# A state-space scan with its chunk states packed by group: 128x256 states, products as two half matmuls

## The chip, the cores and the metric

One Trainium2 chip, one of its NeuronCores. The metric is the device time of one execution of the whole program in microseconds, lower is better. The engines are named as in the profile: PE (TensorE matmul) and PEld (its weight load), DVE (VectorE), ACT (ScalarE), POOL (GpSimd), SP (SyncE, which issues the DMAs).

## The reference, cut to what matters

The reference is a two-layer block of a generator: adaLN-modulated norm, one input projection for four parallel mixers (attention, short convolution, pooling, a bidirectional state-space scan), a gated merge, an output projection, and a gated ConvFFN. 512 latent and 256 context tokens, 1024 channels, all in float32. The change lies in the scan over chunks of 128 tokens (8 heads of 64 channels in 2 groups of 4, a state of 64 per group):

```python
def ssd_scan(x, dt, a_rate, bm, cm, h0):
    ...
    decay_to_end = jnp.exp(a_cum[..., -1:] - a_cum)
    states = jnp.einsum('bcsgn,bcgrs,bcsgrp->bcgrpn', bc, decay_to_end, xdt)
    chunk_decay = jnp.exp(a_cum[..., -1])

    def step(h, inp):
        st, dec = inp
        return h * dec[..., None, None] + st, h
    ...
    y_off = jnp.einsum('bclgn,bcgrpn,bcgrl->bclgrp', cc, h_prev, jnp.exp(a_cum))
    y = (y_diag + y_off).reshape(b, l, nh, p)
```

Each group has its own `bc` and `cc` (64 values per token) and its own four heads: a state of group 0 meets only `cc` of group 0.

## The kernel before, in words

Activations lie with channels on partitions and tokens along the free axis. Every projection (`mm`, lines 124 to 138) is made of three fp32r matmuls per 128 channels, high and low halves of both operands, in segments of 512 latent and 256 context tokens; the 128x1024 weight tiles are fetched by SP and split by ACT and DVE (`split`, line 93).

A layer runs in stages: attention beside the projections of the other mixers, then the scan (`ssd_main`, line 758) beside the merge of the three finished branches, then the scan's gate and norm (`ssd_gate`), then the merge of the scan's branch, the output projection and the ConvFFN. Layer 0 has context and latent outputs, layer 1 latent outputs alone. `interleave` (line 46) writes the two programs of a stage alternately: after each step of the scan it writes as much merge work as the step's `yield` states (10 or 9 us). The tile framework then orders the instructions of every engine by a timeline of its own, so neighbours in the program need not be neighbours on an engine. Every engine runs its list in order.

The scan has two parts. `ssd_chunk` (line 685) makes what lies within a chunk: `cb` (lines 690 to 693, one f32 matmul per group with 64 rows, the partitions of that group), the decays `e` from masks that POOL multiplies (`pm`), and `y`. `ssd_dir` (line 726), once for each direction and in lockstep, carries the state `hs` from chunk to chunk:

- `st` (line 744) is `bt` of the chunk (128 tokens by 128 columns: two groups of 64) times `xe` (128 tokens by 512: all heads), one f32 128x512 matmul. Of its four blocks of 64x256 two are wanted, group 0 with heads 0 to 3 and group 1 with heads 4 to 7; the others mix groups.
- `hs` (lines 745 to 754) is a 128x512 tile that POOL sets to zero; then, for each group, DVE takes the wanted 64x256 block, decays the old state and adds the new one. The zeros stand in the blocks that mix groups.
- `yo` (line 734) is `cT` of the chunk (128 rows, both groups) times `hs`, one f32 128x512 matmul, in which the zeros keep the groups apart. DVE scales it by `ex` into `yot` and adds that to `y`.

There are 10 `st` and 10 `yo` in layer 0, 10 and 8 in layer 1. `yo` shares the two PSUM buffers of tag `a` with `e`, `st` the two of tag `b` with `cb`.

Of the kernel before, what the change touches and what calls it, by code (L numbers as in the profile page):

```python
# [15 lines left out]
P = 128  # L16
# [13 lines left out]
# columns of the packed constants  # L30
C_ID, C_ONE, C_LE, C_GE, C_GT, C_LT, C_EDGE = 0, 128, 256, 384, 512, 640, 768
C_N = 768 + 4 * 2 * 8
# columns of a layer's packed per-channel parameters
Q_NM, Q_NF, Q_CS, Q_FC, Q_XW, Q_XB, Q_PS, Q_SN, Q_BM = 0, 8, 16, 28, 160, 178, 184, 188, 192
Q_N = 192 + 48
# columns of a layer's packed row parameters
# [9 lines left out]
def interleave(main, side):  # L46
    """Trace main; after each of its steps trace as much of side as the TensorE time (us) that the step leaves free."""
    owed = 0.0
    for want in main:
        owed += want  # L50
        while owed > 0:
            got = next(side, None)
            if got is None:
                break
            owed -= got


def mixed(main, side, start, every):
    """main with a step of side after each `every` of its steps from the `start`th on, then the rest of side."""
# [7 lines left out]
class Kernel:  # L67
# [3 lines left out]
    # ---------------------------------------------------------------- helpers  # L71
# [21 lines left out]
    def split(self, hi, lo, src):  # L93
        """src = hi + lo, each of them exact in float32r."""
# [16 lines left out]
    def banks(self, **bufs):  # L111
        """The PSUM banks of a phase: mm for the projections, the other tags for what runs beside them."""
# [11 lines left out]
    def mm(self, w, mov, segs):  # L124
        """w.T @ mov for each token segment: [(first token, tokens, PSUM [P, tokens])]."""
# [17 lines left out]
    def transposes(self, src, tiles, exact=False, tag="b"):  # L143
        """Blocks of P columns of src, each transposed: [(first block, blocks, PSUM [P, blocks * P])].

        exact: src holds float32r values, which one pass moves."""
# [23 lines left out]
    def rows_rstd(self, pool, chunks, n, inv, eng=None, rb=None, ss=None):  # L170
        """1/rms over the channels (chunks on partitions), the same on every partition: PSUM [P, n]."""
# [53 lines left out]
    # ------------------------------------------------------------- modulation  # L225
    def first_norm(self):
        """h of the first layer: its shift on TensorE (the weights stationary), its scale on VectorE."""
# [66 lines left out]
    def mod_steps(self, l, p, conds, pool, bufs=2):  # L294
        """One modulation part on VectorE: rows of the weight scaled per partition and summed, then across partitions."""
# [30 lines left out]
    # -------------------------------------------------------------- attention  # L326
# [13 lines left out]
    def token_major(self, l, mt, segs, ap_):  # L340
        """A projected tile of P channels, transposed: [(first token tile, tiles, PSUM)]."""
# [7 lines left out]
    def heads_ready(self, l, mt, segs, tabs, ap_):  # L349
        """A projected pair of heads, token-major, RMS-normed, gained and rotated: SBUF [P, tiles * 2 heads, 64]."""  # L350
# [803 lines left out]
```

## Time and profile before

| | |
|---|---|
| device time, 3 runs | 2596.28, 2597.34 (median), 2598.14 us |
| span of the profiled execution | 2597.0 us, 34788 instructions (its device time is not listed apart from the three) |
| PE busy | 2520.1 us (97%) |
| PEld | 2144.5 us (83%) |
| DVE | 1684.6 us (65%) |
| ACT | 1002.4 us (39%) |
| POOL | 102.3 us (4%) |
| mean granted TensorE clock | 0.989 |

The profile shows one execution. Busy shares are means over all stages. A matmul's record begins when its weights or columns begin to go in, and the records of consecutive matmuls overlap, so what a matmul costs PE is read from the distance between the starts of records, not from their durations. An f32 matmul leaves two records, an fp32r one a single record. The chain of waits follows the work that ended last back through what released it; the waits say which engine an instruction waited for.

### The profile page before, as it was taken

The page shows a single profiled execution, that of the slowest core. Times are in us where ns is not written, and L with a number is a line of the kernel's source. Part 1 is how long each engine was busy: PE and PEld are TensorE (multiplying, and loading weights), DVE is VectorE, ACT ScalarE, POOL GpSimd, SP SyncE. Part 2 cuts the span into 40 slices and gives each one's busy share as a digit, 9 for nine tenths or more (in the row PEclk, how much of TensorE's full clock was granted, in tenths as well). Part 3 has the DMA queues.
Part 4 walks back from the last instruction along what each step waited for, and adds up shares of the span by engine and source line. Part 5 has one row for each costly group of instructions (what it writes and reads, how often), then busy time and mean ns, then how long its engine had stood idle before and what let it go on. Part 6 is the DMA issues. An engine that isn't in the chain of part 4 may idle for free.

```text
span 2597.0 us, 34788 instructions
## 1 busy us (share of the span) xinstructions
PE 2520.1 (97%) x13684; PEld 2144.5 (83%) x13684; DVE 1684.6 (65%) x2857; ACT 1002.4 (39%) x1717; POOL 102.3 (4%) x125
## 2 busy tenths in 40 slices
PE   7999999999999999999999989999999999899998
PEld 4878888887888888888888878888777788788887
DVE  5666564568689667787765576666478544655656
ACT  3465555431312233232223344665542333333332
POOL 0000000242000000000000000000042000000000
PEclk9999999999999999999999999999999999999999
DMA  6212222331566242344432242132332533233232
GB/s 234 66 33 96 68 68 80 93 105 42 170 196 195 83 138 73 114 152 140 143 111 73 68 144 66 39 104 94 98 106 77 179 110 105 69 107 98 89 102 70
DMA packets 92819, 272.21 MB, mean 105 GB/s; under 512 B 9968, under 2 KB 15600, under 8 KB 91504
## 3 DMA queue, kind: packets, MB, share of 16 engines
q1 hardware_dynamic: 92656, 269.99, 32.4%
q8 instruction: 108, 1.77, 0.3%
q14 instruction: 55, 0.45, 0.1%
HBM read 248.71 MB, written 21.23 MB: 104 GB/s over the span
## 4 chain that ended last, share of the span: by engine, by line
PE 89%; DVE 5%; DMA 2%; ACT 2%; issue 1%; SPq 0%; DVEq 0%; ACTq 0%
PE mm L134 26%; PE mm L135 26%; PE mm L136 26%; PE tp L152 3%; PE s L434 2%; PE ov L449 2%; PE modrow L274 1%; DVE wl L73 1%; ACT wh L95 1%; DMA braw<-bout 1%; PE yo L734 1%; PE st L744 1%; PE e L714 1%; PE y L721 0%; DMA wraw<-w_out 0%
## 5 line engine op out<-in xcount | busy, mean ns | idle before, releaser
L134 PE MATMUL mm<-hh,wh 128*128 128x512 f32 (+1 forms) x2648 | 946.9, 358 | 7.4 <-ACT hh L208 5.9
L135 PE MATMUL mm<-hl,wh 128*128 128x512 f32 (+1 forms) x2648 | 945.7, 357 | 1.4 <-DVE hl L76 1.3
L136 PE MATMUL mm<-hh,wl 128*128 128x512 f32 (+1 forms) x2648 | 941.4, 356 | 1.4 <-DVE wl L73 1.4
L95 ACT CAST wh<-wraw 128x1024 fp32r<-128x1024 f32 (+5 forms) x384 | 350.9, 915 | 748.3 <-PE mm L135 635.5
L73 DVE TENSOR_TENSOR wl<-wraw,wh 128x1024 fp32r<-128x1024 f32 (+5 forms) x384 | 411.9, 1073 | 280.2 <-ACT wh L95 275.3
L134 PEld LDWEIGHTS mm<-hh,wh 128*128 128x128 f32 x2648 | 503.4, 190 | 81.1 <-ACT hh L208 8.0
L135 PEld LDWEIGHTS mm<-hl,wh 128*128 128x128 f32 x2648 | 503.2, 190 | 72.6 <-issue 3.1
L136 PEld LDWEIGHTS mm<-hh,wl 128*128 128x128 f32 x2648 | 502.9, 190 | 72.4 <-DVE wl L73 3.2
L76 DVE SCALAR_TENSOR_TENSOR fc<-mm,par,fc 128x511 f32<-128x511 f32 (+1 forms) x264 | 172.9, 657 | 64.0 <-ACT fc L490 61.3
L134 PE MATMUL mm<-ah,wh 128*128 128x512 f32 (+1 forms) x576 | 196.8, 343 | 2.4 <-ACT ah L95 1.0
L135 PE MATMUL mm<-al,wh 128*128 128x512 f32 (+1 forms) x576 | 196.5, 342 | 0.9 <-DVE al L73 0.9
L136 PE MATMUL mm<-ah,wl 128*128 128x512 f32 (+1 forms) x576 | 196.2, 342 | 0.0
L76 DVE SCALAR_TENSOR_TENSOR x<-mm,mod,x 128x512 f32<-128x512 f32 (+1 forms) x128 | 80.1, 632 | 118.7 <-PE mm L136 118.5
L76 DVE SCALAR_TENSOR_TENSOR macc<-mraw,cond,macc 128x1024 f32<-128x1024 f32 x112 | 141.0, 1280 | 12.9 <-DMA mraw<-w_modk 12.8
L136 PE MATMUL mm<-bh,wl 128*128 128x512 f32 (+1 forms) x384 | 137.4, 359 | 1.7 <-DVE wl L73 1.6
L135 PE MATMUL mm<-bl,wh 128*128 128x512 f32 (+1 forms) x384 | 138.5, 361 | 0.4 <-DVE bl L73 0.4
L134 PE MATMUL mm<-bh,wh 128*128 128x512 f32 (+1 forms) x384 | 137.9, 361 | 0.2 <-ACT bh L95 0.2
L134 PEld LDWEIGHTS mm<-ah,wh 128*128 128x128 f32 x576 | 110.3, 192 | 15.7 <-ACT ah L95 1.4
L490 ACT ACTIVATE fc<-mm,par 128x512 f32<-128x512 f32 (+1 forms) x132 | 80.8, 612 | 109.4 <-PE mm L136 109.4
L135 PEld LDWEIGHTS mm<-al,wh 128*128 128x128 f32 x576 | 110.6, 192 | 13.2 <-DVE al L73 1.4
L136 PEld LDWEIGHTS mm<-ah,wl 128*128 128x128 f32 x576 | 110.3, 192 | 12.1
L73 DVE TENSOR_TENSOR pt<-tp,pt 128x256 fp32r<-128x256 f32 (+1 forms) x144 | 76.9, 540 | 52.9 <-ACT pt L95 51.4
(253 smaller groups left out, 2921.2 us busy)
## 6 DMA issues: line engine op xcount, KB each, us to landing
wraw<-w_up SPq DMA_DIRECT2D x88, 512.0 KB, 3.5
mraw<-w_modk SPq DMA_DIRECT2D x80, 512.0 KB, 3.9
wraw<-w_in SPq DMA_DIRECT2D x64, 512.0 KB, 3.5
wraw<-w_gate SPq DMA_DIRECT2D x64, 512.0 KB, 3.5
wraw<-w_branch SPq DMA_DIRECT2D x64, 256.0 KB, 2.9
wraw<-w_down SPq DMA_DIRECT2D x40, 320.0 KB, 3.0
wraw<-w_out SPq DMA_DIRECT2D x24, 512.0 KB, 3.5
mraw<-w_modm SPq DMA_DIRECT2D x8, 1024.0 KB, 11.2
```

Of the source, the lines that this page charges most:

```text
L73: return (eng or self.nc.vector).tensor_tensor(out=out, in0=in0, in1=in1, op=op)
L76: return self.nc.vector.scalar_tensor_tensor(out=out, in0=in0, scalar=scalar, in1=in1, op0=op0, op1=op1)
L95: self.nc.scalar.copy(hi, src)
L134: self.nc.tensor.matmul(out, lhsT=a, rhs=x0, start=(k == 0), stop=False)
L135: self.nc.tensor.matmul(out, lhsT=a, rhs=x1, start=False, stop=False)
L136: self.nc.tensor.matmul(out, lhsT=b, rhs=x0, start=False, stop=(k == nk - 1))
L152: self.nc.tensor.transpose(tp[:, j * P : (j + 1) * P], src(lo + j), self.identr if exact else self.ident)
L274: nc.tensor.matmul(rows[:32, p * 256 : (p + 1) * 256], lhsT=cond[:, k], rhs=raws[b][:, k, p * 256 : (p + 1) * 256], start=(k == 0), stop=( ...
L434: nc.tensor.matmul(sc[:, t0 : t0 + n], lhsT=qT[:, h, i * P : (i + 1) * P], rhs=self.kT[g][:, part, t0 : t0 + n], start=(part == 0), stop=( ...
L449: nc.tensor.matmul(ov, lhsT=self.v[:, kc, g].rearrange("p a d -> p (a d)"), rhs=pt[j][:, c].rearrange("p h q -> p (h q)"), start=(j == 0 a ...
L490: nc.scalar.activation(o, s, AF.Copy, scale=w1)
L714: nc.tensor.matmul(e, lhsT=self.maskr[:, d * P : (d + 1) * P], rhs=pm.rearrange("p h q -> p (h q)"), start=(n == 0), stop=(n == 3))
```

## The change

The state of a direction becomes 128x256: group 0 on partitions 0 to 63, group 1 on 64 to 127, with no zeros. The product `st` becomes two matmuls, one per group, with 64 output columns and 256 columns of `xe`, into the two partition halves of one PSUM tile. `yo` becomes two matmuls of 64 rows and 256 columns, each into a PSUM buffer of its own. POOL's memset goes. The state's decay and addition are one DVE instruction each of 128x256 where there were two of 64x256; `yot` is made by two of 128x256 where there was one of 128x512. The decays are copied once per layer into `eg`, in which each partition half holds its own group's (`ssd_decays`, two small ACT copies). Comments and docstrings also went from the file; empty lines stand in their place, so that line numbers behind `ssd_chunk` are shifted.

```diff
+    def ssd_decays(self, sp):
+
+        self.eg = sp.tile([P, 2, 6, 4], F32, name="eg", tag="eg", bufs=1)
+        for g in range(2):
+            r = slice(64 * g, 64 * g + 64)
+            self.nc.scalar.copy(self.eg[r], self.ex[r, 4:6, :, 4 * g : 4 * g + 4])
+
     def ssd_dir(self, l, d, with_ctx, sp):
...
             if hs is not None and (with_ctx or c < 4):
-                yo = self.aux("a", 512, "yo")
-                nc.tensor.matmul(yo, lhsT=self.cT[:, c * P : (c + 1) * P], rhs=hs, start=True, stop=True)
+                yo = [self.aux("a", 256, "yo") for _ in range(2)]
+                for g in range(2):
+                    r = slice(64 * g, 64 * g + 64)
+                    nc.tensor.matmul(yo[g], lhsT=self.cT[r, c * P : (c + 1) * P], rhs=hs[r], start=True, stop=True)
                 t = sp.tile([P, 512], F32, name="yot", tag="es", bufs=2)
-                self.tt(self.heads(t), self.heads(yo), self.bc(self.ex[:, d, c]), ALU.mult)
+                for g in range(2):
+                    ex = self.ex[:, d, c, 4 * g : 4 * g + 4]
+                    self.tt(self.heads(t[:, 256 * g : 256 * g + 256]), self.heads(yo[g]), self.bc(ex), ALU.mult)
                 self.tt(self.y[:, c], self.y[:, c], t, ALU.add)
...
-            st = self.aux("b", 512, "st")
-            nc.tensor.matmul(st, lhsT=self.bt[:, c], rhs=xe, start=True, stop=True)
-            new = sp.tile([P, 512], F32, name="hs", tag=f"hs{d}", bufs=2)
-            nc.gpsimd.memset(new, 0.0)
+            st = self.aux("b", 256, "st")
             for g in range(2):
-                r, q = slice(64 * g, 64 * g + 64), slice(256 * g, 256 * g + 256)
-                if hs is None:
-                    nc.vector.tensor_copy(new[r, q], st[r, q])
-                else:
-                    dec = self.ex[r, 4 + d, c, 4 * g : 4 * g + 4]
-                    self.tt(new[r, q].rearrange("p (h e) -> p h e", e=64), hs[r, q].rearrange("p (h e) -> p h e", e=64), dec[:, :, None].to_broadcast([64, 4, 64]), ALU.mult)
-                    self.tt(new[r, q], new[r, q], st[r, q], ALU.add)
+                r = slice(64 * g, 64 * g + 64)
+                nc.tensor.matmul(st[r], lhsT=self.bt[:, c, r], rhs=xe[:, 256 * g : 256 * g + 256], start=True, stop=True)
+            new = sp.tile([P, 256], F32, name="hs", tag=f"hs{d}", bufs=2)
+            if hs is None:
+                nc.vector.tensor_copy(new, st)
+            else:
+                self.tt(self.heads(new), self.heads(hs), self.bc(self.eg[:, d, c]), ALU.mult)
+                self.tt(new, new, st, ALU.add)
             hs = new
...
         for c in (4, 5, 0, 1, 2, 3) if with_ctx else range(4):
             self.ssd_chunk(l, c, sp)
             yield 10.0
+        self.ssd_decays(sp)
         for _ in zip(*[self.ssd_dir(l, d, with_ctx, sp) for d in range(2)]):
             yield 9.0
```

How the instructions stand on PE, in layer 0's scan. Rows give line, operation, output<-inputs, shape; `mm` are the merge's projections, x2 is two in a row. First the middle of the scan, before:

```order
L134 MATMUL mm<-hh_101,wh 128x256
L135 MATMUL mm<-hl_102,wh 128x256
L734 MATMUL yo<-hs,cT 128x512
L744 MATMUL st<-xe,bt 128x512
L136 MATMUL mm<-hh_101,wl 128x256
L134 MATMUL mm<-hh_103,wh 128x256
```

The same place after the change:

```order
L136 MATMUL mm<-hh_103,wl 128x256
L760 MATMUL st<-xe,bt 64x256 x2
L746 MATMUL yo<-hs,cT 128x256
L134 MATMUL mm<-hh_105,wh 128x256
L135 MATMUL mm<-hl_106,wh 128x256
L136 MATMUL mm<-hh_105,wl 128x256
L134 MATMUL mm<-bh,wh 128x512
L746 MATMUL yo<-hs,cT 128x256
L135 MATMUL mm<-bl,wh 128x512
```

The two halves of `st` stand together, the two of `yo` with four projections between them. Over the whole program 16 of the 20 `st` pairs stand together and 4 have another matmul between their halves; of the 18 `yo` pairs none stands together. In eight places an `st` half or pair stands directly beside a `yo` half, as here. A little further on in layer 0 a split `st` pair, after the change:

```order
L134 MATMUL mm<-bh,wh 128x256
L135 MATMUL mm<-bl,wh 128x256
L760 MATMUL st<-xe,bt 64x256
L746 MATMUL yo<-hs,cT 128x256
L760 MATMUL st<-xe,bt 64x256
```

A half of `yo` has come between the halves of `st`; its partner stands further down.

## Rows read from the trace of the kernel before

**Rows 1.** The page: span, and PE's busy time with its instructions.
```profile
span 2597.0 us, 34788 instructions
...
PE 2520.1 (97%) x13684; PEld 2144.5 (83%) x13684; DVE 1684.6 (65%) x2857; ACT 1002.4 (39%) x1717; POOL 102.3 (4%) x125
```

**Rows 2.** The page: the chain that ended last, shares of the span by line.
```profile
PE mm L134 26%; PE mm L135 26%; PE mm L136 26%; PE tp L152 3%; PE s L434 2%; PE ov L449 2%; PE modrow L274 1%; DVE wl L73 1%; ACT wh L95 1%; DMA braw<-bout 1%; PE yo L734 1%; PE st L744 1%; PE e L714 1%; PE y L721 0%; DMA wraw<-w_out 0%
```

**Rows 3.** Stretches: length, busy us of PE, PEld, DVE, ACT, POOL; clock, DMA share, GB/s.
```profile
580.00:660.00 80.00, 80.00 (x413) 63.17 (x412) 66.58 (x122) 17.90 (x37) 18.47 (x20) 1.00 0.18 54
1950.00:2020.00 70.00, 68.80 (x287) 51.07 (x286) 60.06 (x100) 17.87 (x31) 15.59 (x16) 1.00 0.25 72
```

**Rows 4.** PE's waits, 1895 to 2150 us: who for whom, total, times, longest.
```profile
PE mm L136 <- DVE wl L73: 1.6, 1, 1.6
PE st L744 <- DVE xe L73: 1.2, 1, 1.2
```

**Rows 5.** Timeline of SP, layer 1: scan's result stored, first load of the next merge.
```profile
2057.86 0.46 SPq L786 DMA_DIRECT2D bout<-gt  x1
...
2099.61 0.33 SPq L808 DMA_DIRECT2D braw<-bout  x1
```

**Rows 6.** Timeline of PE, layer 0, around one `st`: start, length, tile, shape.
```profile
590.15 0.28 PE L136 MATMUL mm<-hh,wl 128*128 128x256 f32 x1
590.27 1.02 PE L744 MATMUL st<-xe,bt 128*128 128x512 f32 x2
590.72 0.68 PE L134 MATMUL mm<-hh,wh 128*128 128x256 f32 x1
591.24 0.28 PE L135 MATMUL mm<-hl,wh 128*128 128x256 f32 x1
```

**Rows 7.** The tile `yo`: count, duration in ns (min/median/max), first and last start.
```profile
L734 PE MATMUL yo<-hs,cT x36: 590/591/594, 610.3 to 2015.5; 128*128 128x512 f32 x36
L73 DVE TENSOR_TENSOR yot<-yo,ex x18: 683/688/693, 618.3 to 2016.9; 128x512 f32<-128x512 f32 x18
```

**Rows 8.** Timeline of PE, layer 0, around a lone `cb` of 64 rows.
```profile
520.72 0.28 PE L136 MATMUL mm<-bh,wl 128*128 128x256 f32 x1
520.92 0.49 PE L693 MATMUL cb<-cT,bT 64*128 64x128 f32 x2
521.34 0.50 PE L714 MATMUL e<-pm,maskr 128*128 128x512 f32 x1
```

**Rows 9.** Timeline of PE, fp32r matmuls with 32 output columns beside a full one.
```profile
52.81 0.39 PE L570 MATMUL mm<-hh,wd 128*32 128x512 f32 x1
53.04 0.39 PE L134 MATMUL mm<-hh,wh 128*128 128x512 f32 x1
```

**Rows 10.** Timeline of PE, layer 0, around two `cb` directly behind each other.
```profile
499.22 0.28 PE L136 MATMUL mm<-hh,wl 128*128 128x256 f32 x1
499.43 0.49 PE L693 MATMUL cb<-cT,bT 64*128 64x128 f32 x4
499.85 0.73 PE L714 MATMUL e<-pm,maskr 128*128 128x512 f32 x2
```

**Rows 11.** Timeline of PE behind f32 matmuls with 32 output columns.
```profile
49.85 1.89 PE L274 MATMUL modrow<-mraw,cond 128*32 128x256 f32 x8
51.67 0.39 PE L134 MATMUL mm<-hh,wh 128*128 128x256 f32 x1
51.90 0.39 PE L570 MATMUL mm<-hh,wd 128*32 128x512 f32 x1
```

**Rows 12.** The tile `hs`: count, duration in ns (min/median/max), first and last start.
```profile
L73 DVE TENSOR_TENSOR hs<-hs,ex x32: 406/422/1261, 593.5 to 2000.0; 64x256 f32<-64x256 f32 x32
L73 DVE TENSOR_TENSOR hs<-hs,st x32: 401/419/426, 605.7 to 2010.5; 64x256 f32<-64x256 f32 x32
L746 POOL MEMSET hs<- x20: 524/526/531, 488.8 to 1996.1; 128x512 f32 x20
L750 DVE COPY hs<-st x8: 409/422/428, 591.4 to 1957.1; 64x256 f32<-64x256 f32 x8
```

## The prediction, made before the changed kernel ran

> **What bounds the kernel now.** I read the page first: PE is busy for 97% of the span [rows 1], and in the chain of waits three quarters of the span are the projections of `mm`, while the two matmuls that are edited hold 1% each [rows 2]. The table of stretches then covers the two places where the chunk scan runs (580 to 660 us in layer 0, 1950 to 2020 us in layer 1): PE is busy for 80.0 of 80 and for 68.8 of 70 us, at a granted clock of 1.00, and VectorE for 83% and 86% [rows 3]. Beside the scan PE always has projections of the merge to run, so the scan is paid for in PE time and not in latency. Two views bear that out. PE's waits: from 1895 us on it waited 1.6 us once for a weight's low half and 1.2 us once for `xe`, both VectorE [rows 4]; in layer 0's scan stretch there is no wait. And the scan's result is stored in layer 1 by 2058 us but first read at 2099.6 us [rows 5], 41 us later, so a later chain of states delays nobody. What counts is how much PE time the same work takes after the edit.
>
> **What a state or output product costs now.** It is one f32 128x512 matmul, in the trace two records. Between the matmul record before `st` at 590.27 and the first regular one after it at 591.24 lie 0.97 us; 0.12 of that is the 128x256 `mm` that came in between (590.15 to 590.27 is that shape's step), so 0.85 us for 512 columns [rows 6]. A record of `yo` lasts the same 0.59 us [rows 6, 7]. There are 20 `st` (40 records in pairs) and 18 `yo` [rows 7]: 17.0 + 15.3 = 32.3 us of PE. Per 256 columns that is 0.43 us, per 128 it is 0.21.
>
> **The change, part by part.**
>
> **Output products.** Each becomes two matmuls with 64 rows and 256 columns, 0.43 us of columns each. The trace has such half-height matmuls already: `cb`, 64 rows by 128 columns. Alone between full-height ones, it starts 0.20 us after the record at 520.72 (0.12 is usual, so 0.08 late), the next record starts at 521.34 and lasts 0.50 us [rows 8] where 0.39 is usual [rows 9]. So 521.34 - 520.72 - 0.12 + 0.11 = 0.61 us for a product with 0.21 us of columns: 0.40 us goes into changing to half height and back. Two `cb` directly behind each other go from 499.22 to 499.85, with 0.73 us for the two records behind them [rows 10] (usual is 0.23 + 0.39 = 0.62 [rows 9]): 0.63 - 0.12 + 0.11 = 0.62 us for both. They run side by side, and the second costs nothing. A pair of `yo` halves side by side would thus take 0.43 + 0.40 = 0.83 us, against 0.85 now: even the best case gains nothing. But the order of the change shows that none of the 18 pairs stays together; full-height matmuls stand between the halves in every one. So each of the 36 halves pays alone: 36 x 0.83 = 29.9 against 15.3 us, **+14.6 us**. That is the term on which the forecast rests; its price is from eight `cb` that stand alone, all within 0.01 us.
>
> **State products.** Each becomes two matmuls with 64 output columns, one per half of the PSUM partitions. In the order 16 of 20 pairs stand together, 4 are split. Two prices are unknown. First, switching: after the f32 `modrow` with 32 output columns, eight records of 256 columns (8 x 0.21 = 1.71 us) begin at 49.85, and the next record begins 1.82 us later, 0.11 late, and then takes 0.23 us to the following one instead of 0.12 [rows 11]: 0.2 us to leave. The way in has no clean row; I take 0.14 (the same drain and half the weight columns), 0.34 in all. The ends: nothing, since fp32r matmuls with 32 output columns pass to a full one at the usual step of 0.23 us [rows 9], and 0.40 as for `cb`. I take 0.34, as `modrow` is f32 like `st`. Second, whether the two run side by side. No row has two column halves; the nearest is the `cb` pair [rows 10], which does, so I take 0.43 us for a pair; the other end is 0.85. The sum: 24 groups (16 pairs, 8 lone halves) x (0.43 + 0.34) = 18.5 against 17.0 us, **+1.5 us**. One after the other it would be +8.3, without a switching cost -6.7. The Trainium skill ("TensorE: Matmul & The Clock Gate", section "Measured speedup vs the span model") gives 2.38 times for three column tiles; my estimate from that is some 13% more than one for a pair, which would add 0.9 us to the sum, and no run here shows it.
>
> In eight places a lone `st` half or pair and a `yo` half stand directly beside each other, and one of the two changes is saved: 8 x 0.2 = **-1.6 us**.
>
> **VectorE.** The 32 decays and 32 additions of 64x256 become 16 and 16 of 128x256, at the 0.42 us that a 256-wide one takes now, and the 8 copies become 4 [rows 12]: -15.1 us. The 18 `yot` of 0.688 us [rows 7] become 36 of 256 columns, estimated at the same 0.42: +2.7. So 12.4 us less, over two layers, on an engine that PE waits for little. What it can give back is the 2.8 us of rows 4; PE also comes later at these places, so I take half, **-1.4 us**, with 0 and -2.8 as ends.
>
> **The rest at nothing.** 20 memsets of 0.53 us leave POOL [rows 12]; PE took none of its waits from them. Two small ScalarE copies (`eg`) come in each layer before the scan of the states; ScalarE is busy for 18 of 70 to 80 us there [rows 3], and uncovered they would cost about 1 us. No DMA is added; those that shift wait for the scan's end, with the 41 us of rows 5.
>
> **Sum:** 14.6 + 1.5 - 1.6 - 1.4 = +13.1 us on a span of 2597.0; the median of the runs, 2597.3, lies 0.3 us above that. **2610.4 us**, 0.5% slower. About 0.2% (5.2 us) is what a measurement can tell from no change.
>
> **The rivals.**
> - *Column halves run one behind the other.* +6.8 us for 16 pairs: 2617. For it: no row shows two of them at once. Against: `cb`.
> - *Column halves switch for free*, as the fp32r rows do [rows 9]: 24 x 0.34 = -8.2, less the shared changes that then fall away (+1.6): 2604. Against: `modrow` is the f32 case [rows 11].
> - *No difference to be measured.* Free switching, both VectorE waits gone (1.4 us more) and a lone `yo` half 0.1 us cheaper than rows 8 make it (36 x 0.1): 2610.4 - 6.6 - 1.4 - 3.6 = 2599. Against: three errors in one direction.
> - *Faster: halves run side by side at no price of change.* Then 20 and 18 products drop from 0.85 to 0.43 us each, -16 us, 2581. It decides from the point where split halves still overlap and a change costs less than 0.42 - 5.2 / 38 = 0.28 us. Rows 8 speak against the first and the written order against the second. The Trainium skill ("TensorEngine Tiling (Array Packing)", section "Theoretical Speedup") gives up to 2 times for such halves; by that rule the kernel would gain, and the same page's "Key Properties" has the drain at a mode change that rows 8 price.
> - *A new wait.* A `yo` pair now takes both PSUM buffers of tag `a`, which the `e` of the chunks use too; PE stops in order until VectorE has read a half (0.42 us). At 36 halves and up to 0.4 us each, +14 more: 2625. Against: projections stand between most pairs, and VectorE has less to do than before.
>
> **How the numbers follow.** Forecast (2605 to 2615): 0.57. One behind the other (to 2620): 0.17. Free switching (2601 to 2605): 0.10. No difference: 0.07. Faster: 0.04. New wait (above 2620): 0.05. The range 2601 to 2620 holds 0.84 of it. Slower by over 0.2%, beyond 2602.5: 0.57 + 0.17 + 0.05 + most of the free switching, 0.86; within 0.2%: 0.10; faster: 0.04.
>
> **What would show it.** Right: in the trace after, a lone `yo` half with about 0.08 us before it, and a record behind it that takes 0.10 us longer than usual; from the matmul before to the second one after, 0.8 us more than their own steps. `st` pairs whose four records come as two pairs of starts a few ns apart (side by side), or at four separate times (one behind the other). VectorE's busy time down by about 12 us while the span grows. Wrong: `yo` halves without a gap before them, or VectorE as the engine that PE waits for in the scan stretches, with more than 5 us in its waits.

## The result, and the profile after

The changed kernel takes 2616.27 us (median of 4 runs, 2611.88 to 2620.61), against 2597.74 (2596.28 to 2598.99) for the kernel before beside it: 18.5 us longer by the medians; the ratio with its 95% interval is 1.0078 [1.0064, 1.0091]. The forecast was 13.1 us longer, 2610.4 with a range of 2601 to 2620. The sign held, and the time lies in the range, though above the band of 2605 to 2615 that the forecast kept for itself; the size fell short by 5 us. Medians and ranges in this document leave out four executions (one of the changed kernel, two of variants, one of the kernel before) that took 2817 to 6410 us.

The page of the changed kernel, span and engines:

```profile
span 2618.7 us, 34868 instructions
...
PE 2536.9 (97%) x13760; PEld 2145.7 (82%) x13760; DVE 1670.8 (64%) x2839; ACT 1004.3 (38%) x1721; POOL 94.8 (4%) x105
```

Beside [rows 1] the span grows by 21.7 us and PE's busy time by 16.8, while VectorE loses 13.8 (the forecast said 12.4), and POOL 7.5. An engine was relieved that was not the limit.

The stretches of [rows 3] in the changed kernel (length; busy us of PE, PEld, DVE, ACT, POOL; clock, DMA share, GB/s):

```profile
580.00:660.00 80.00, 80.00 (x417) 59.09 (x415) 52.30 (x101) 17.79 (x38) 16.49 (x14) 1.00 0.13 40
1950.00:2020.00 70.00, 69.31 (x315) 48.71 (x314) 53.14 (x92) 21.07 (x41) 19.10 (x15) 1.00 0.27 81
```

PE is as full as before. VectorE drops from 66.6 to 52.3 us in the first stretch and PE has no gap that this could have closed.

The tiles `yo`, `st` and `hs` (count, ns min/median/max, first and last start), which answer to [rows 7, 12]:

```profile
L746 PE MATMUL yo<-hs,cT x72: 376/428/480, 611.2 to 2043.0; 64*128 64x256 f32 x72
L73 DVE TENSOR_TENSOR yot<-yo,ex x36: 417/425/426, 618.7 to 2043.4; 128x256 f32<-128x256 f32 x36
...
L760 PE MATMUL st<-xe,bt x80: 379/404/431, 591.7 to 2018.7; 128*64 128x256 f32 x80
...
L73 DVE TENSOR_TENSOR hs<-hs,eg x16: 407/416/1264, 593.3 to 2018.9; 128x256 f32<-128x256 f32 x16
L73 DVE TENSOR_TENSOR hs<-hs,st x16: 403/415/422, 605.2 to 2019.8; 128x256 f32<-128x256 f32 x16
L763 DVE COPY hs<-st x4: 409/414/425, 592.4 to 1971.7; 128x256 f32<-128x256 f32 x4
```

VectorE's price goes by the 256 elements per partition and not by the 64 or 128 partitions: 0.42 us in both kernels. The last `yo` starts at 2043.0 instead of 2015.5; 15 us of that had gathered before layer 1's scan begins (table below), the rest are the scan's own delay and a later place in the order.

The timeline of PE in layer 0 around a lone `yo` half, as [rows 8] showed it for `cb`:

```profile
610.86 0.28 PE L134 MATMUL mm<-hh,wh 128*128 128x256 f32 x1
610.97 0.28 PE L135 MATMUL mm<-hl,wh 128*128 128x256 f32 x1
611.18 0.70 PE L746 MATMUL yo<-hs,cT 64*128 64x256 f32 x2
611.81 0.50 PE L714 MATMUL e<-pm,maskr 128*128 128x512 f32 x1
612.14 0.28 PE L136 MATMUL mm<-hh,wl 128*128 128x256 f32 x1
```

Read the starts. From the `mm` at 610.97 to the one at 612.14 there are 1.17 us; 0.12 belongs to the first `mm` and 0.23 to `e`, so 0.82 us are the half's. The small signs are there too: 0.21 before it where 0.12 is usual, and 0.33 behind `e` where 0.23 is. Over the trace 31 lone halves could be measured so, median 0.82 us. The forecast took 0.83 from `cb`, a whole 512-column product took 0.85 before.

A pair of `st` halves that stands together, and further on in the same scan one that is split by an `e`, both from the timeline of PE in the changed kernel:

```profile
591.45 0.28 PE L136 MATMUL mm<-hh,wl 128*128 128x256 f32 x1
591.66 0.65 PE L760 MATMUL st<-xe,bt 128*64 128x256 f32 x4
592.24 0.38 PE L134 MATMUL mm<-hh,wh 128*128 128x256 f32 x1
592.46 0.28 PE L135 MATMUL mm<-hl,wh 128*128 128x256 f32 x1
...
614.20 0.65 PE L760 MATMUL st<-xe,bt 128*64 128x256 f32 x2
614.77 0.49 PE L714 MATMUL e<-pm,maskr 128*128 128x512 f32 x1
615.20 0.65 PE L760 MATMUL st<-xe,bt 128*64 128x256 f32 x2
```

From 591.45 to 592.46 there are 1.01 us, less 0.12 each for the two `mm` it is 0.77; the median of 13 such pairs is 0.78 (forecast: 0.77). Four records of `st` take 0.65 us in all, exactly what two records of a lone half take below: the column halves run side by side. Their starts lie at 591.657, .664, .924 and .932. The two lone halves around `e` can be priced together: from the `mm` before them to the second `mm` behind them,

```profile
613.99 0.28 PE L135 MATMUL mm<-hl,wh 128*128 128x256 f32 x1
...
616.00 0.28 PE L134 MATMUL mm<-hh,wh 128*128 128x256 f32 x1
```

there are 2.01 us; less 0.12 twice for `mm` and 0.23 for `e`, 1.54 are left, 0.77 for each half. A lone half costs what a pair does, as the forecast had it.

Where an `st` half stands directly beside a `yo` half, part of this is saved. The clearest place lies in layer 1:

```profile
2016.91 0.39 PE L136 MATMUL mm<-hh,wl 128*128 128x512 f32 x1
2017.22 0.65 PE L760 MATMUL st<-xe,bt 128*64 128x256 f32 x2
2017.80 0.70 PE L746 MATMUL yo<-hs,cT 64*128 64x256 f32 x2
2018.43 0.65 PE L760 MATMUL st<-xe,bt 128*64 128x256 f32 x2
2019.00 0.50 PE L134 MATMUL mm<-hh,wh 128*128 128x512 f32 x1
2019.34 0.40 PE L135 MATMUL mm<-hl,wh 128*128 128x512 f32 x1
```

From 2016.91 to 2019.34 there are 2.43 us, 1.97 without the two `mm` of 0.23. Three lone halves apart would take 0.77 + 0.82 + 0.77 = 2.36, so each of the two neighbourings saves 0.2 us.

PE's waits in layer 1, which answer to [rows 4] (1895 to 2160 us, the two that the scan or the merge beside it shows):

```profile
PE mm L134 <- ACT wh L95: 2.2, 2, 1.9
PE mm L136 <- DVE wl L73: 1.8, 2, 1.1
```

Before, the same view has, beside one of 0.2 us, a line that [rows 4] does not show:

```profile
PE mm L134 <- ACT wh L95: 1.2, 2, 0.7
```

The wait for `xe` is gone, and weights take its place: 4.0 us in all in both profiles (before: 1.6 + 1.2 + 1.2). Between these two executions nothing was given back. In the second executions of both programs, reported below, the same sums are 6.2 us before (1.8 of it for `xe`) and 4.4 in the changed kernel, so up to 1.8 us may have been.

To [rows 5] answers this in SP's timeline of the changed kernel (loads of the scan's gate; the scan's result stored; the first load of the merge that reads it):

```profile
2044.28 2.37 SPq L785 DMA_DIRECT2D gt<-zkeep  x4
...
2079.01 2.44 SPq L799 DMA_DIRECT2D bout<-gt  x4
...
2120.43 0.33 SPq L821 DMA_DIRECT2D braw<-bout  x1
```

The scan of layer 1 ends 21 us later than before, about as much later as the merge's own projections, and still 39 us lie between its store and the load that reads it. The slack held here.

### The profile page after: what moved, and what is told of

Its sections match the earlier page's. It is cut to its first block, busy times and chain, and to the rows that moved or that the text cites. A ratio compares the mean times of both kernels' runs of the same rounds, so it can differ in the third digit from the quotient of the medians.

```text
span 2618.7 us, 34868 instructions
## 1 busy us (share of the span) xinstructions
PE 2536.9 (97%) x13760; PEld 2145.7 (82%) x13760; DVE 1670.8 (64%) x2839; ACT 1004.3 (38%) x1721; POOL 94.8 (4%) x105
## 4 chain that ended last, share of the span: by engine, by line
PE 87%; DVE 6%; DMA 3%; ACT 2%; issue 1%; SPq 0%; DVEq 0%; ACTq 0%
PE mm L134 25%; PE mm L135 25%; PE mm L136 25%; PE tp L152 3%; PE ov L449 2%; PE s L434 2%; DVE wl L73 1%; PE modrow L274 1%; DMA braw<-bout 1%; PE yo L746 1%; DMA mraw<-w_modk 1%; ACT wh L95 1%; PE e L714 1%; DMA wraw<-w_down 1%; DVE macc L76 1%
## 5 line engine op out<-in xcount | busy, mean ns | idle before, releaser
L136 PEld LDWEIGHTS mm<-ah,wl 128*128 128x128 f32 x576 | 109.0, 189 | 13.8 <-DVE wl L73 1.8
```

What stands on the lines that cost most here:

```text
L136: self.nc.tensor.matmul(out, lhsT=b, rhs=x0, start=False, stop=(k == nk - 1))
```

## Where the time lies

A tally of both traces says where the span grew. Each kernel has the same 11436 `mm` matmuls of projections; the start of the k-th in one trace less its start in the trace of before is the delay so far, and the table gives what each stretch (in the time of before) adds, in us. Four programs were profiled twice, which shows how far such numbers repeat.

| profiled execution | to 581 | layer 0 scan, to 716 | to 1840 | attention's end of layer 1, to 1953 | layer 1 scan, to 2047 | to 2581 | total |
|---|---|---|---|---|---|---|---|
| changed | +1.4 | **+8.2** | +5.0 | +0.6 | **+5.7** | +0.8 | +21.6 |
| changed, again | -1.7 | **+8.2** | +2.2 | -0.5 | **+6.1** | +1.0 | +15.2 |
| pairs in a critical section | -1.1 | +5.9 | -1.5 | +1.9 | +12.4 | -0.6 | +17.0 |
| `st` halves only | +0.3 | +0.1 | +0.8 | -0.3 | +3.2 | +0.5 | +4.5 |
| `yo` halves only | +0.1 | +6.9 | +2.3 | +0.7 | +9.1 | +0.9 | +20.0 |
| pairs kept by order | -0.6 | -1.2 | +1.3 | +5.0 | +6.6 | -0.6 | +10.6 |
| pairs kept by order, again | -0.6 | -0.6 | +0.5 | +4.9 | +4.8 | +0.5 | +9.6 |
| packed, full height | -1.7 | 0.0 | +2.5 | +3.5 | -1.9 | -0.3 | +2.1 |
| one shape change | -3.5 | -1.8 | +0.9 | +1.9 | +9.9 | +0.8 | +8.2 |
| layer 0 alone | +0.6 | -2.4 | +2.3 | +5.2 | +0.6 | +0.9 | +7.1 |
| layer 0 alone, again | -5.3 | -1.7 | +1.0 | +3.2 | +0.5 | 0.0 | -2.4 |
| before, again | -2.0 | 0.0 | -1.6 | -0.2 | +4.2 | -0.2 | +0.3 |

Layer 0's scan repeats within 0.7 us, and there the change costs 8.2 us in both executions; the forecast's prices for that layer (20 lone `yo` halves, 13 groups of `st`, five shared changes, less 20 full products) give 16.6 + 10.0 - 1.0 - 17.0 = 8.6. Layer 1's is less sure: against the first execution of before the change costs 5.7 and 6.1 (priced 5.9, the rest of the 14.5 of the three terms), but before itself took 4.2 us more there the second time, with PE waiting for `xe` and weights; against that execution the change costs only 1.5 and 1.9 us there. The other columns scatter by some us between executions of one program (5.9 in the first, up to 3 in the others), and runs of one kernel spread by up to 14 us (before: 2589.23 to 2602.84).

## The experiments

All of them compute the same output as the changed kernel; none leaves work out. The kernel before ran beside each group on the same chip: 2596.24, then 2596.23, 2594.07 and 2596.24 us.

**The change, once more, in five rounds.** No edit.

> The changed kernel once more, timed in five rounds. Theory (PE pays about 0.4 us whenever it changes to half matmuls and back, and nearly every yo half changes alone): the scan stretches cost +13 to +14 us against the kernel before, so a run at 2611 to 2613 us is the plain cost, and the runs at 2620 hold some 8 us from outside the scan that are not there every time; both levels should come again. Rival (the change makes the whole program 18 us slower, by waits that it leads to further down): all runs near 2616 to 2620, and the extra time stands in the same places in every profile.

Measured: 2617.52 us (2614.03 to 2620.49), ratio 1.0083 [1.0064, 1.0101], 21.3 us longer. Neither expectation held whole. The scans cost 14.3 us, as the theory had it, but the four runs (2614.0, 2616.5, 2618.6, 2620.5) show no two levels and none at 2611 to 2613. Against the rival, the time outside the scans is not the same in both profiles: 7.7 us in the execution that took 2620.61, 0.9 in the one of 2614.03. The profiled execution repeats layer 0's 8.2 us and layer 1's 6 us. In the merge behind layer 0's scan (735 to 1010 us) PE waits 8.3 us in all, 7.5 in the kernel before and 9.7 in the first profile of the change: some of what lies outside the scans are new short waits for gates and weights, but no more than 1 to 2 us of it could be named.

**Both halves of `yo` together, by a critical section.**

```diff
-                for g in range(2):
+                with self.tc.tile_critical():
+                  for g in range(2):
                     r = slice(64 * g, 64 * g + 64)
                     nc.tensor.matmul(yo[g], lhsT=self.cT[r, c * P : (c + 1) * P], rhs=hs[r], start=True, stop=True)
```

> Only the order is changed: the two halves of each yo are issued directly behind each other, all else as in the changed kernel. Theory (cost of changing, paid once per pair, halves side by side): a yo pair takes 0.83 us of PE instead of 1.64 for two lone halves, 18 times 0.81 = 14.6 us less, and all st pairs stand together as well, 2 to 3 us less: 2593 to 2598 us, about the kernel before or a little faster. Rival (a yo pair needs both PSUM buffers and PE waits for VectorE to free them): this order needs both at the same moment, so 2612 us or more.

Measured: 2614.74 us (2613.4 to 2616.3), ratio 1.0073 [1.0055, 1.009]: not what was expected. The timeline of PE in layer 0 tells why (the bracket is idle time before the record, and what ended it):

```profile
630.54 0.28 PE L136 MATMUL mm<-hh,wl 128*128 128x256 f32 x1
631.26 0.70 PE L747 MATMUL yo<-hs,cT 64*128 64x256 f32 x4 [0.44 <-issue]
632.20 0.70 PE L761 MATMUL st<-xe,bt 128*64 128x256 f32 x4 [0.24 <-issue]
632.84 0.50 PE L134 MATMUL mm<-bh,wh 128*128 128x512 f32 x1
```

The halves do run side by side (four records in 0.70 us, which a lone half takes for its two), but PE stands idle 0.44 us before the pair and 0.24 behind it, with nothing to wait for that the profile shows. The section itself costs most of what the pairing saves (0.68 us here, of 0.81 expected). So this run separates nothing, and the pairs had to be brought together in another way (below).

**Only the state products as halves.** `yo`, `hs` of 128x512, the memset and the two decays stay as before; `st` and the addition that reads it are as in the change.

```diff
-            st = self.aux("b", 512, "st")
-            nc.tensor.matmul(st, lhsT=self.bt[:, c], rhs=xe, start=True, stop=True)
+            st = self.aux("b", 256, "st")
+            for g in range(2):
+                r = slice(64 * g, 64 * g + 64)
+                nc.tensor.matmul(st[r], lhsT=self.bt[:, c, r], rhs=xe[:, 256 * g : 256 * g + 256], start=True, stop=True)
...
-                    self.tt(new[r, q], new[r, q], st[r, q], ALU.add)
+                    self.tt(new[r, q], new[r, q], st[r], ALU.add)
```

> Only st as two half matmuls; the state is zero-padded 128x512 and yo one full matmul as in the kernel before, VectorE's work as before. Theory: 19 st pairs together at 0.78 us and 2 lone halves, against 20 at 0.85: 2596 to 2598 us, no difference from the kernel before. Rival (column halves are the dear part): 8 us or more above the kernel before, 2605 us.

Measured: 2602.38 us (2594.56 to 2605.26), ratio 1.0017 [1.0005, 1.0029]: 4 us above what was expected, 3 below the rival. In layer 0 nine of ten pairs stand together and one is split, so 11 x 0.78 - 10 x 0.85 = +0.1 us by the prices, and the scan takes 0.1 us more. The 3.2 us in layer 1 come with PE waits for weights (2.4 us for `wh`, 2.3 for `wl`), and lie within what before itself differs there.

**Only the output products as halves.** The state is packed, `st` is one full matmul again, and each group's addition reads its block.

```diff
-            st = self.aux("b", 256, "st")
-            for g in range(2):
-                r = slice(64 * g, 64 * g + 64)
-                nc.tensor.matmul(st[r], lhsT=self.bt[:, c, r], rhs=xe[:, 256 * g : 256 * g + 256], start=True, stop=True)
+            st = self.aux("b", 512, "st")
+            nc.tensor.matmul(st, lhsT=self.bt[:, c], rhs=xe, start=True, stop=True)
```

> Only yo as half matmuls with the packed 128x256 state; st is one full 128x512 matmul, of which VectorE takes the two wanted blocks. In this order 32 yo halves stand alone and 2 pairs together. Theory: 32 times 0.82 plus 2 times 0.83 = 27.9 us against 15.3, +12.6 us of PE, about 1 us back from VectorE: 2607 to 2611 us. Rival (st is the dear part): 2597 us.

Measured: 2614.73 us (2610.96 to 2618.81), ratio 1.0073 [1.0054, 1.0092], 18.5 us: nearly the whole loss, and more than the 2607 to 2611 expected. Layer 0's scan costs 6.9 (18 lone halves and one pair: 18 x 0.82 + 0.83 - 10 x 0.85 = 7.1 by the prices); of the 9.1 in layer 1, 2.1 are a wait of PE's transposes of `y` for the gate's tile `gt`. The output halves are the dear part.

**Pairs kept together by the order.** Output halves were split because the second one waits for its own PSUM buffer of tag `a`. Here the first half also waits for the last reader of that tag, so that both can start when the first does; no idle section is needed.

```diff
-            nc.scalar.activation(es.rearrange("p h q -> p (h q)"), e, AF.Exp)
+            self.freed = nc.scalar.activation(es.rearrange("p h q -> p (h q)"), e, AF.Exp)
...
-                    nc.tensor.matmul(yo[g], lhsT=self.cT[r, c * P : (c + 1) * P], rhs=hs[r], start=True, stop=True)
+                    ins = nc.tensor.matmul(yo[g], lhsT=self.cT[r, c * P : (c + 1) * P], rhs=hs[r], start=True, stop=True)
+                    if g == 0:
+                        self.tc.add_manual_dep(ins.ins, self.freed.ins.name, mybir.DependencyInfo(mybir.DependencyClass.Sync, mybir.DependencyReason.DATA), reason="both buffers")
...
-                    self.tt(self.heads(t[:, 256 * g : 256 * g + 256]), self.heads(yo[g]), self.bc(ex), ALU.mult)
+                    self.freed = self.tt(self.heads(t[:, 256 * g : 256 * g + 256]), self.heads(yo[g]), self.bc(ex), ALU.mult)
```

> The changed kernel with one dependency more: the first yo half also waits until the second one's PSUM buffer is free, so that in the order all 18 yo pairs and all 20 st pairs stand together, without the section that cost PE 0.4 to 0.6 us before each pair in the run with the halves together. Theory (changing the array's shape is paid per group, halves side by side): 18 x 0.83 + 20 x 0.78 = 30.5 us of PE against 32.3 in the kernel before and some 46 in the changed one; 14 to 16 us faster than the changed kernel, 2595 to 2602 us. Rival (both buffers at once make PE wait, or packing in itself is slow): 2610 us or more.

Measured: 2607.35 us (2603.13 to 2609.4), ratio 1.0042 [1.0028, 1.0056], between the two expectations. All 18 `yo` pairs and all 20 `st` pairs stand together now. The timeline of PE in layer 0 shows the first, and in layer 1 the transposes of `y` behind the scan:

```profile
618.29 0.40 PE L135 MATMUL mm<-hl,wh 128*128 128x512 f32 x1
618.61 0.70 PE L746 MATMUL yo<-hs,cT 64*128 64x256 f32 x4
619.25 0.50 PE L136 MATMUL mm<-hh,wl 128*128 128x512 f32 x1
...
2037.87 1.04 PE L152 MATMUL tp<-const,y__17454 128*128 128x128 f32 x8
2043.44 1.97 PE L152 MATMUL tp<-const,y__17454 128*128 128x128 f32 x8 [4.53 <-DVE gt L76]
```

A `yo` pair costs 0.83 us (median of 17), an `st` pair 0.78 (19): by these, 38 x 0.85 of before become 18 x 0.83 + 20 x 0.78, 1.8 us less over both layers. Layer 0's scan is 1.2 us shorter than before where the change made it 8.2 longer: **9.4 us in one layer were the split pairs**, of `yo` and of `st`, shown by an edit that only adds the dependency that closes them. By the prices it should be 9.6: ten `yo` halves less (8.3), three `st` groups less (2.3), and five shared changes that fall away (-1.0). "Up to twice as fast" is not to be had at 256 columns per half: the Trainium skill ("TensorEngine Tiling (Array Packing)", section "Theoretical Speedup") gives up to 2 times for two such halves, and the second half is indeed free here, but 0.40 us of changing shape stands against the 0.43 us that it saves.

In layer 1 the kernel loses 6.6 us, and the second row of `tp` shows most of it: PE stands 4.53 us for `gt`. VectorE, which must empty the transposes' PSUM into `gt`, waits for its load:

```profile
2042.69 1.39 DVE L76 SCALAR_TENSOR_TENSOR gt<-gt,tp 128x512 f32<-128x512 f32 x2 [4.41 <-DMA gt<-zkeep]
```

SP issues the loads from `zkeep` at 2033.89, with the first transposes at 2037.87; before, the loads were issued at 2018.53 and the transposes ran at 2022.80 and 2030.04, 7.2 us apart, with projections between the two groups. Here the second group stands directly behind the first, and PE, in order, can do nothing else.

**The same, with full-height output products.** From the kernel with only output halves: `cz` holds `cT` once per group, with the other group's rows zero, so each half of `yo` is a 128-row matmul of 256 columns, and there is no change of shape.

```diff
+        self.cz = sp.tile([P, 2, T], F32, name="cz", tag="cz", bufs=1)
+        self.nc.gpsimd.memset(self.cz, 0.0)
+        for g in range(2):
+            r = slice(64 * g, 64 * g + 64)
+            self.nc.scalar.copy(self.cz[r, g, :n], self.cT[r, :n])
...
-                    nc.tensor.matmul(yo[g], lhsT=self.cT[r, c * P : (c + 1) * P], rhs=hs[r], start=True, stop=True)
+                    nc.tensor.matmul(yo[:, 256 * g : 256 * g + 256], lhsT=self.cz[:, g, c * P : (c + 1) * P], rhs=hs, start=True, stop=True)
```

> The packed 128x256 state without any half matmul: yo is two full-height matmuls of 256 columns whose weights are copies of cT with the other group's rows zero, st one full 128x512 matmul. Theory: the array's shape never changes for them, so PE pays 0.85 us per product as before, VectorE 7 us less: 2594 to 2600 us, no difference from the kernel before. Rival (the packed state, its decays or the shifted order of the engines cost the time, not the shape of the matmuls): 2608 us or more.

Measured: 2602.01 us (2600.86 to 2603.05), ratio 1.002 [1.001, 1.003]. The scans cost 0.0 and -1.9 us, with the same packed state, the same number of output matmuls and nearly the same VectorE work (1674 us, and 1679 there) as the kernel with only output halves, which lost 18.5. In the scans the packing costs nothing. In this order 16 of the 18 products have both halves together, so the scans' time does not yet tell height from separation. The four lone halves do; two of them stand around an `e`:

```profile
608.52 0.28 PE L134 MATMUL mm<-hh,wh 128*128 128x256 f32 x1
608.64 0.59 PE L750 MATMUL yo<-hs,cz 128*128 128x256 f32 x2
608.88 0.59 PE L714 MATMUL e<-pm,maskr 128*128 128x512 f32 x1
609.30 0.59 PE L750 MATMUL yo<-hs,cz 128*128 128x256 f32 x2
```

From 608.52 to 609.30 there are 0.78 us, less 0.12 and 0.23 it is 0.43, the price of the columns alone, where a lone half of 64 rows costs 0.82. So neither the split nor, by the run before, the half height of a closed pair is dear, but a half-height product that stands alone. The time missed its range by 2 us: 3.5 us were lost at the end of layer 1's attention, where nothing was edited (see the last section).

**One change of shape per step.** As the pairs by order; in addition the `st` pair stands directly behind the `yo` pair, which for that waits for `xe` too.

```diff
+            if n < 5:
+                xe = sp.tile([P, 512], F32, name="xe", tag="xe", bufs=1)
+                made = self.tt(self.heads(xe), self.heads(self.xs[:, c]), self.bc(self.cf[d][:, c]), ALU.mult)
...
+                    if g == 0:
+                        dep(ins, self.freed, mybir.DependencyClass.Sync)
+                        if n < 5:
+                            dep(ins, made, mybir.DependencyClass.Sync)
...
+                if last is not None:
+                    dep(ins, last, mybir.DependencyClass.NoSync)
```

> As the run with all pairs together, and the yo pair of a step directly followed by the st pair of the same step, so that one of the two changes of shape falls away: 15 changes fewer at 0.2 us, 3 us of PE less than with pairs apart. Theory: 2592 to 2599 us if PE is what bounds. Rival (the yo pair now waits for xe as well, so the chain of states gets longer and layer 1's scan ends after the merge work beside it has run out): 3 to 10 us slower than with pairs apart, with PE idle before the transposes of y in layer 1.

Measured: 2608.91 us (2606.97 to 2612.99), ratio 1.0052 [1.004, 1.0065]. Layer 0's scan is 1.8 us shorter than before, layer 1's 9.9 longer, with PE's waits there:

```profile
PE tp L152 <- DVE gt L76: 7.7, 1, 7.7
PE tp L152 <- DVE y__17454 L73: 1.6, 1, 1.6
```

In this order 13 `yo` pairs have an `st` pair directly behind them, and layer 0's scan is about 1 us shorter than with the pairs apart. In layer 1 there are 9.3 us of waiting in front of the transposes: the rival with the longer chain was right about the place, though the whole is only 1.6 us slower than with the pairs apart, where it said 3 to 10.

**Layer 0 alone.** The scan of layer 0 as in the last kernel, that of layer 1 as in the kernel before.

```diff
-        self.ssd_decays(sp)
-        for _ in zip(*[self.ssd_dir(l, d, with_ctx, sp) for d in range(2)]):
+        if l == 0:
+            self.ssd_decays(sp)
+        for _ in zip(*[(self.ssd_dir if l == 0 else self.ssd_dir_old)(l, d, with_ctx, sp) for d in range(2)]):
```

> Layer 0 as in the run with one change of shape (yo pair followed by st pair), layer 1's scan as in the kernel before, with its 128x512 zero-padded state. Theory (the pairs are worth 2 to 4 us of PE in layer 0; in layer 1 PE stood still before the transposes of y since the chain of states ended after the merge work beside it): layer 1's scan shift falls from +10 us to within 1 us, layer 0's stays at -2 to -4, the merge behind it keeps some 2 us of new waits: 2593 to 2598 us, no difference from the kernel before. Rival (what the runs with all pairs lost does not hang on layer 1's chain, but on the pairs or the packed state): 2603 us or more.

Measured: 2602.09 us (2595.64 to 2606.61), ratio 1.0026 [1.0012, 1.004]. Layer 1's scan falls from +9.9 to +0.6 and the wait for `gt` is gone, layer 0's stays at -2.4: both by the theory. The time missed its range by 4 us; 5.2 us were lost at the end of layer 1's attention.

**Three repeats, for that end of attention.** The last kernel, the pairs kept by order, and the kernel before, once more.

> The same program as in the run of layer 0 alone, once more. The question is whether the 5.2 us that it lost at the end of layer 1's attention (1840 to 1953 us, with a granted clock of 0.77 in 1880 to 1910) belong to its order of instructions or differ from run to run. Theory, the order: the clock of 1880 to 1910 is again below 0.85, the stretch again 4 to 6 us longer than in the kernel before, and the median again 2600 to 2604. Rival, from run to run: the clock there is 0.94 to 1.00, the stretch within 2 us of the kernel before, and this profiled execution takes 2594 to 2600.

> The kernel with its pairs kept together by the order, once more. Theory, the order: the granted clock of 1880 to 1910 is again below 0.85 (it was 0.77), and PE again waits 4 to 5 us in front of the transposes of y at 2035 to 2045 us. Rival, from run to run: the clock there is 0.94 or more; the wait for the gate stays, since it comes of the order of the scan.

> The kernel before, once more. Theory, the order: the granted clock of 1880 to 1910 is again 1.00. Rival, from run to run: it is below 0.95. In both cases the scans keep their times within 1.5 us of the first profile: the start of the projections beside them at 581, 716, 1953 and 2047 us moves by the same amount at both ends of each scan.

Measured: layer 0 alone 2599.76 us (2595.65 to 2603.63), ratio 1.0014 [1.0004, 1.0024], and in its profile 3.2 us lost there with a clock of 0.89, between what the theory and the rival had said, while its profiled execution took 2596.40 us, as the rival had it; pairs by order 2608.36 in one execution, 4.9 us lost there with a clock of 0.77, and PE again waits 4.0 us for `gt`; before 2599.06 in one execution, a clock of 1.00, nothing lost there. The expectation that before's scans keep their times held for layer 0 (0.0) and failed for layer 1 (+4.2). No version beat the kernel before.

## Why the prediction was right, and where it fell short

- **PE bounds the scan: right.** PE is busy for 80.0 of 80 us in both kernels, and 13.8 us less of VectorE's work could not shorten a stretch in which PE never waited.
- **Output halves, +14.6: right in price and cause.** 0.82 us per lone half, measured 31 times, against 0.83. The kernel with only these halves has nearly the whole loss, full-height halves have none in the scans and cost 0.43 us when alone, and closing the pairs, of `yo` and `st`, takes 9.4 us out of layer 0's scan.
- **State halves, +1.5: right.** 0.78 us per pair against 0.77, side by side, and 0.77 per lone half. The surcharge for a pair of column tiles, 0.9 us in all, that the forecast estimated from the 2.38 times of the Trainium skill ("TensorE: Matmul & The Clock Gate", section "Measured speedup vs the span model") is not to be seen: a pair costs no more than a lone half. With 0.43 us of columns, 0.35 are left for the change; the forecast's 0.34, in which the 0.14 for the way in had no row, came out. With `st` alone as halves layer 0's scan moved by 0.1 us.
- **Neighbours that share a change, -1.6: right.** 0.2 us saved at each, measured where `st`, `yo` and `st` stand in a row. With it, the scans' sum of prices is 14.5, and they measured 13.9 and 14.3 against the first execution of before. Layer 0's part, 8.2 of 8.6, is firm; that layer 1's comes out so well (5.7 and 6.1 of 5.9) is partly luck, as against the second execution of before it would be 1.5 and 1.9.
- **VectorE's give-back, -1.4: open.** The forecast's list of waits left out the 1.2 us for `wh`. The wait for `xe` vanished in both executions of the change, but between the first profiles the waits for weights' halves grew by as much, so that nothing was gained; between the second ones 1.8 us were. That a weight's way through load, ACT and VectorE bound those places, and not VectorE's load from the scan, is suggested by the names of the waits and not shown.
- **The rest at nothing: the term that was too small.** Outside the scans the two profiled executions of the change lie 7.7 and 0.9 us behind the first of before (21.6 - 13.9 and 15.2 - 14.3). If the scans cost in the median run what they cost there, the medians leave 4.6 and 7.0 us (18.5 - 13.9 and 21.3 - 14.3). Most of it shows between 716 and 1840 us (5.0 and 2.2), with 0.8 and 1.0 in the tail. New waits of PE behind layer 0's scan, 2.2 and 0.8 us, are part of it. What the remainder is made of stays open: before's own second execution differs from its first by 3.9 us outside the scans.
- **The 41 us of slack [rows 5]: right for the change (39 us), and too simple as an argument.** It looked at who reads the scan's result at last. The pairs by order show another reader: the transposes of `y`, which sit in PE's list at a fixed place and wait there for the gate's loads. In the kernel before and the changed one that wait is hidden, in four of the variants it costs 2.1 to 7.7 us.
- **The rivals.** One behind the other, and free switching, both fell by the `st` pair; halves side by side at no price by the lone `yo` half, and no difference to be measured, which needed free switching, with it. A new wait through tag `a`: PE's waits show none for `yo`. The time came out beside the 2617 of the first of these, without its mechanism.

## What to carry to other kernels

A lone product of half the rows or half the columns saved next to nothing here: 0.77 to 0.82 us for 256 columns, where the whole product of 512 took 0.85. Changing the shape of the array and back cost 0.35 to 0.40 us, as much as 210 to 240 columns of f32 by these prices, so halves must stand at least in pairs before they pay. By the same prices longer runs of halves would pay more, which was not tried beyond two pairs in a row. Before packing tiles to relieve VectorE, look whether PE waits for it at all, and see in the order of the changed program whether the pairs stay together: two buffers that come free at different times were enough to part them here. And where one engine works through its list in order, the slack of a late result counts to the first instruction on that engine that touches it, not to the last reader.

## What the runs showed of the hardware beyond that

The granted clock at the end of layer 1's attention. Four executions of the stretch 1880 to 1910 us (columns as in the stretches above), first the kernel before:

```profile
1880.00:1910.00 30.00, 24.70 (x126) 18.81 (x126) 19.84 (x43) 15.34 (x35) 8.45 (x10) 1.00 0.21 62
```

The changed kernel:

```profile
1880.00:1910.00 30.00, 22.85 (x131) 19.25 (x130) 15.86 (x32) 18.56 (x39) 2.04 (x2) 0.94 0.11 36
```

The pairs kept by order, repeated:

```profile
1880.00:1910.00 30.00, 25.34 (x106) 20.27 (x106) 17.81 (x39) 13.94 (x34) 4.12 (x4) 0.77 0.12 36
```

Layer 0 alone, repeated:

```profile
1880.00:1910.00 30.00, 26.65 (x124) 21.08 (x123) 17.35 (x38) 11.92 (x28) 10.13 (x12) 0.89 0.22 71
```

What matters is the third number from the right, the clock: 1.00, 0.94, 0.77 and 0.89, where full is 2.4 GHz and the other level 1.2. The stretch is fixed in time, and the programs reach the same work up to some 20 us apart, so it does not hold all of a fall in each: layer 0 alone, repeated, has 0.96 in the 40 us ahead of it too. Around here PE waits in every kernel, some 7 us in gaps of up to 1.9 us, and before shows that the clock need not fall for that. Which waits these are goes with the program's order: in six executions of four programs (before, changed, each of the two products alone) the longest sum is `ov` for VectorE's `pt` with 2.6 us, and the clock is 0.94 to 1.00; in seven of five programs it is 1.9 to 2.4 us of `tp` for `aT` or as much of `s` for `pr`, and it is 0.77 to 0.94. Within the seven, 0.94 goes with 1.9 us more in that part of the table above, 0.89 and 0.83 with 3.2 and 3.5, 0.77 with 4.9 to 5.2. With layer 0 alone edited, 1200 us earlier, that is a loss where nothing was touched. How the edit moves these waits, and why the clock falls more behind the one set than behind the other, was not tried. That it belongs to the order rather than to chance is likely and not shown: it rests on the two sets, which meet at 0.94, and on two repeats, which gave 0.77 after 0.77 and 0.89 after 0.77, so its size does change from run to run. The clock of whole executions points the same way: 0.984 or 0.985 in all five runs of the pairs by order, 0.986 to 0.988 in all 16 of layer 0 alone, 0.987 to 0.990 in the kernel before beside them.

Two column halves of one f32 product start 7 ns apart, and the next matmul starts 0.58 us after the first, the same as behind one half alone. Two row halves do the same, with 0.63 us.
